# Second part of the output projection in single PSUM banks, later turns of the first group's kept heads, and sample values in slabs

## Chip, cores and metric

The kernel runs on one core of a Trainium2 chip. The metric is the device time of one execution, in microseconds (us). Lower is better.

## The reference, cut to what matters

One decoder layer is computed in fp32 for 2048 prompt tokens and for a sample group of 8 sequences with 8 tokens each; both share the weights. Four retention heads and four HGRN2 heads each carry a state through chunks of 64 tokens; the outputs of the eight heads go through one output projection, the input is added, and a feed-forward part follows.

```python
def mixer(h, pos, s_ret, s_hg, w_in, ret_norm_w, hgrn_norm_w, lb, w_out):
    proj = h @ w_in
    rq, rk, rv, rg, hq, hf, hi, hg = jnp.split(proj, idx, axis=-1)
    ...
    o_r, s_ret_new = chunk_gla(rq, rk, rv, log_g_ret, s_ret)
    o_r = (head_rmsnorm(o_r, ret_norm_w) * gate_r).reshape(B, T, RET_W)
    ...
# chunk_gla, per chunk and head
    o = jnp.einsum('bhts,bhsv->bhtv', A, vb) + jnp.einsum('bhtd,bhdv->bhtv', qb * jnp.exp(b), S)
    S_new = S * jnp.exp(b_last[:, :, 0, :])[..., None] + jnp.einsum('bhsd,bhsv->bhdv', k_dec, vb)
```

The mixer's result is the two groups of heads side by side, times `w_out`; the layer adds its input to it.

## The kernel before

All tokens are cut into three groups: group 0 holds the 64 sample tokens and 512 prompt tokens (T = 576), groups 1 and 2 hold 768 prompt tokens each. A group goes through the mixer in four passes p = 0 to 3, each with one retention head and one HGRN2 head, then through the output projection; the feed-forward part of all groups comes last.

Every fp32 product is made of three matmuls: both operands are cut into a high part and a rest (`hi`, `lo`), and high by high, high by rest and rest by high are added up in PSUM. The cast on ScalarE (ACT) that makes `hi` is L306, the subtraction on VectorE (DVE) that makes `lo` is L314. The matmuls of the plain projections are L448 in `proj`; those of the block products with kept operands are L1844, which `matmul` counts.

PSUM has eight banks. While the mixer runs, the pool `pj` has two buffers of two banks each for the big products, and the pool `mm` has four buffers of one bank for all small ones. After the mixer of the last group the pool `pf` (two buffers of two banks) stands where `mm` was. `tile2()` hands out two buffers of `pf`, then two of `pj`, in turn.

**The output projection** (`out_proj`) of a group has two parts. The first (`residual`) takes the heads of passes 0 to 2 beside the last mixer. The second, which the change touches, runs alone on TensorE (PE): for each of eight column blocks, 12 matmuls into one `pj` tile (128x288 in group 0, 128x384 in the others), then one DVE addition to the first part (L1905), one ACT copy with the weight of the norm (L1906), and two stores, `fres` and `fin` (L1908). With two `pj` buffers, a block can start only when the DVE addition of the block two ahead of it has read its tile.

**Kept heads.** The outputs of passes 0 to 2 are stored (`fo`), and in pass 3 `fetch_heads` loads them again and `cut_heads` turns them: transposes on PE (L1833), then the cut in `hi` on ACT (L1834) and `lo` on DVE (L1835). `later(d, f)` runs `f` after d more ticks; a tick comes after every three (`proj`) or two (`matmul`) products. Those numbers and those of `at` in `mixer` set the order in which the code is issued; a scheduler then sets the order on each engine.

**Sample part of group 0.** In each pass, `sample_values` loads the sample rows of the values three times into one tile (six transfers of 32 KB for the two halves, L1315), casts them and subtracts (L1317). `sample_blocks` spreads them (DVE, L1345), `sample_update` multiplies them with the keys (PE, L1357) and adds the product to the old states (DVE, L1361 for retention, L1364 for HGRN2). The old states of both heads are loaded by `sample_states` (L1291, from `ret_s` and `hg_s`) and read by the matmuls L1306. The running state `S` of the prompt is copied by L1696 and read by L1686. `load()` gives one of the six `ld` buffers, `get()` one of the 44 slabs; both are handed on in a fixed order, so a load waits for the last reader of the buffer that it gets. All transfers named here are issued by SyncE's queue (SP), one after the other: an issue that waits holds up those behind it.

Of the kernel before, what the change touches and what calls it, by code (L numbers as in the profile page):

```python
# [9 lines left out]
F32 = mybir.dt.float32  # L10
# [3 lines left out]
ALU = mybir.AluOpType  # L14

P = 128
# [7 lines left out]
H = 4  # L24
# [70 lines left out]
N_ORDER = (0, 1, 4, 5, 2, 3, 6, 7)  # L95
# [110 lines left out]
class Kernel:  # L206
# [7 lines left out]
    def at(self, when, fn, *a):  # L214
        heapq.heappush(self.agenda, (when, self.n_at, fn, a))
        self.n_at += 1
# [219 lines left out]
            out.append(self.blocks.popleft())  # L436
        return out

    def proj(self, g, blocks, acts, pieces=None):

        pieces = pieces or g.pieces
        T2 = pieces[0][1] - pieces[0][0]
        pj = self.pj.tile([P, 2, 512], F32, tag="pj", name="pj")
        n = len(blocks)
        for j, ((wh, wl), (ah, al)) in enumerate(zip(blocks, acts)):
            for q, (w, a) in enumerate(((wh, ah), (wh, al), (wl, ah))):
                for i, (c0, c1) in enumerate(pieces):
                    self.nc.tensor.matmul(  # L448
                        pj[:, i, :T2], w, a[:, c0:c1],
                        start=j == 0 and q == 0, stop=j == n - 1 and q == 2)  # L450
                self.tick()
        return pj[:, :len(pieces), :T2]

    def cut(self, src, hi, lo, T, lag=0):
        self.tc.keep_in_program_order(self.nc.scalar.copy(hi[:, :T], src[:, :T]))
# [452 lines left out]
    def mix(self, g):  # L908
        nc = self.nc
        if g.ns:  # L910
            g.qm = [self.get(), self.get()]
            for q in g.qm:
                nc.gpsimd.memset(q, 0.0)
        g.o, g.oc = {}, {}
        end = 0
        for p in range(H):
            b = {}
            if self.fast and p == H - 1 and g.i + 1 < len(self.groups):
                self.norm_ahead(self.groups[g.i + 1], g.i == 0)
            (self.project_blocks if g.blocks else self.project)(g, p, b)  # L920
            end = self.mixer(g, p, b, max(self.now, end))
            if p == H - 1:
                for q in range(H - 1):
                    if self.fast:
                        self.later((2, 24, 46)[q] if g.ns else (2, 8, 38)[q], self.fetch_heads, g, q)
                        self.later((22, 44, 66)[q] if g.ns else (22, 40, 64)[q], self.cut_heads, g, q)
                    else:
                        self.later((4, 16, 28)[q], self.cut_heads, g, q)
            (self.values_blocks if g.blocks else self.values_direct if self.fast else self.values)(g, p, b)
# [376 lines left out]
                nc.tensor.matmul(po, g.qm[i][:, s * NS:(s + 1) * NS], s0[i][:, s * P:(s + 1) * P],  # L1306
                                 start=False, stop=i == 1 and s == 3)

    def sample_values(self, g, v):

        nc, out = self.nc, []
        for i in range(2):
            r, w = self.load(), self.getr()
            for t in range(3):
                nc.sync.dma_start(r[32 * t:32 * t + 32, :2 * P], v[32 * i:32 * i + 32])  # L1315
            nc.scalar.copy(w[:96, :2 * P], r[:96, :2 * P])
            nc.vector.tensor_tensor(out=w[64:96, :2 * P], in0=r[64:96, :2 * P], in1=w.bitcast(F32)[64:96, :2 * P], op=ALU.subtract)  # L1317
            out.append(w)
        return out
# [62 lines left out]
    def mixer(self, g, p, b, t0):  # L1382


        nc, T, n0 = self.nc, g.T, g.ns
# [352 lines left out]
        def outs(t):  # L1738
            if n0:
                at(t - 24 if fast else t - 14, sample_load, 0)  # L1740
                at(t - 14, sample_turn, 0)
                at(t - 20, lambda: x.update(vw=self.sample_values(g, b["vrows"])))
                for hd in range(2):
                    at(t - 6 + 8 * hd, lambda hd=hd: x.update({("vm", hd): self.sample_blocks(x["vw"], hd)}))
                at(t + 1, sample, 0)
                at(t + 4, sample_state, 0)
                at(t - 14 if fast else t + 6, sample_load, 1)
                at(t + 6, sample_turn, 1)
                at(t + 10, sample, 1)
                at(t + 13, sample_state, 1)  # L1750
                rows = slice(0, NS)
                at(t + 14, squares, "s", 0, -1, rows)
                at(t + 14, factors, "s", 1, rows)
                at(t + 19, gated, "s", 0, -1, rows)
                t += 15
# [140 lines left out]
    def out_proj(self, g, when, beside, between=lambda: None):  # L1896

        nc, T = self.nc, g.T
        part = self.residual(g, when, beside)
        between()  # L1900
        g.res, g.in_ = (self.dp.tile([P, KB, T], F32, name=self.tag + f"{name}{g.i}") for name in ("res", "in"))
        for n in N_ORDER:
            pj = self.proj(g, self.take(2), g.oc[H - 1])
            r, b = part[n], self.get()
            nc.vector.tensor_tensor(out=self.v2(r, g), in0=pj, in1=self.v2(r, g), op=ALU.add)  # L1905
            nc.scalar.activation(b[:, :T], r[:, :T], AF.Copy, scale=self.vec[:, V_FFN + n:V_FFN + n + 1])  # L1906
            for kept, t in ((g.res, r), (g.in_, b)):
                nc.sync.dma_start(kept[:, n], t[:, :T])  # L1908
        self.flush()
# [555 lines left out]
```

## Time and profile before

| | |
|---|---|
| time, median of 3 runs | 2387.14 us (2385.1 to 2387.51) |
| profiled execution, its own time | 2385.61 us |
| its span in the trace | 2383.8 us (1.8 us lie around it) |
| PE busy | 2351.0 us (99%) |
| DVE busy | 1799.2 us (75%) |
| ACT busy | 1230.7 us (52%) |
| GpSimd (POOL) busy | 148.1 us |
| TensorE clock granted | 0.997 |

The trace gives each instruction with its start, its length and, where its engine was idle before it, what ended the idle time. A line number is that of the kernel before. PE is busy nearly throughout, so the idle time of PE in the trace, piece by piece, is the most that a change of order can win. Lengths of neighbours on DVE and PE overlap a little: what one instruction takes of its engine is the distance of two starts.

### The profile page before, as it was taken

The page shows a single profiled execution, that of the slowest core. Times are in us where ns is not written, and L with a number is a line of the kernel's source. Part 1 is how long each engine was busy: PE and PEld are TensorE (multiplying, and loading weights), DVE is VectorE, ACT ScalarE, POOL GpSimd, SP SyncE. Part 2 cuts the span into 40 slices and gives each one's busy share as a digit, 9 for nine tenths or more (in the row PEclk, how much of TensorE's full clock was granted, in tenths as well). Part 3 has the DMA queues.
Part 4 walks back from the last instruction along what each step waited for, and adds up shares of the span by engine and source line. Part 5 has one row for each costly group of instructions (what it writes and reads, how often), then busy time and mean ns, then how long its engine had stood idle before and what let it go on. Part 6 is the DMA issues. An engine that isn't in the chain of part 4 may idle for free.

```text
span 2383.8 us, 39321 instructions
## 1 busy us (share of the span) xinstructions
PE 2351.0 (99%) x15322; PEld 2309.0 (97%) x15322; DVE 1799.2 (75%) x2299; ACT 1230.7 (52%) x1974; POOL 148.1 (6%) x202
## 2 busy tenths in 40 slices
PE   9999999999999999999999999999999999999998
PEld 8888799999999999999999999999999999999997
DVE  8666777767676766758769997666998786669887
ACT  5555565466654555536455555444544364445443
POOL 4212201010001001000000000000000000000000
PEclk9999999999999999999999999999999999999999
DMA  8888778778858777968677665766655457565541
GB/s 291 287 289 282 257 271 336 266 287 288 321 188 316 290 285 265 320 223 292 225 243 271 230 216 181 243 211 226 240 184 191 152 190 261 198 239 177 204 154 69
DMA packets 232505, 575.60 MB, mean 241 GB/s; under 512 B 24179, under 2 KB 92659, under 8 KB 232310
## 3 DMA queue, kind: packets, MB, share of 16 engines
q1 hardware_dynamic: 232166, 572.98, 68.8%
q8 instruction: 122, 2.00, 0.3%
q14 instruction: 73, 0.60, 0.1%
q10 hardware_dynamic: 144, 0.02, 0.0%
HBM read 419.95 MB, written 151.66 MB: 240 GB/s over the span
## 4 chain that ended last, share of the span: by engine, by line
PE 82%; DVE 2%; ACT 1%; issue 0%; DMA 0%; POOL 0%; SPq 0%; DVEq 0%; ACTq 0%; POOLq 0%
PE pj L1844 35%; PE pf L1844 28%; PE pj L1103 9%; PE pj L448 6%; PE mm L1686 1%; PE mm L1684 1%; PE mm L1692 1%; PE mm L1461 0%; PE mm L1614 0%; PE mm L1372 0%; PE mm L1833 0%; DMA lo<-fki0VA12lo 0%; DVE slab L1905 0%; DVE slab L1940 0%; DVE ld L872 0%
## 5 line engine op out<-in xcount | busy, mean ns | idle before, releaser
L1844 PE MATMUL pj<-slab,hi 128*128 128x384 f32 (+1 forms) x3504 | 853.8, 326 | 2.2 <-ACT hi L306 1.0
L306 ACT CAST hi<-raw 128x1024 fp32r<-128x1024 f32 (+1 forms) x449 | 470.8, 1049 | 683.5 <-PE pj L1844 259.1
L314 DVE TENSOR_TENSOR lo<-raw,hi 128x1024 fp32r<-128x1024 f32 (+1 forms) x449 | 548.8, 1222 | 173.8 <-ACT hi L306 159.5
L1844 PE MATMUL pf<-slab,hi 128*128 128x384 f32 (+1 forms) x2768 | 652.4, 321 | 0.0
L1844 PEld LDWEIGHTS pj<-slab,hi 128*128 128x128 f32 x3504 | 614.6, 188 | 3.4 <-ACT slab L1026 1.3
L1844 PE MATMUL pj<-slab,lo 128*128 128x384 f32 (+1 forms) x1752 | 570.4, 326 | 0.0
L1844 PEld LDWEIGHTS pf<-slab,hi 128*128 128x128 f32 x2768 | 480.7, 188 | 0.1
L1844 PE MATMUL pf<-slab,lo 128*128 128x384 f32 (+1 forms) x1384 | 443.1, 320 | 0.0
L1844 PEld LDWEIGHTS pj<-slab,lo 128*128 128x128 f32 x1752 | 329.4, 188 | 0.0
L1103 PE MATMUL pj<-hi,slab 128*128 128x256 f32 x1344 | 263.1, 288 | 2.8 <-DVE slab L1031 1.8
L448 PE MATMUL pj<-slab,hi 128*128 128x288 f32 (+1 forms) x1280 | 257.0, 316 | 5.6 <-DVE slab L1905 3.3
L1844 PEld LDWEIGHTS pf<-slab,lo 128*128 128x128 f32 x1384 | 260.1, 188 | 0.0
L1103 PEld LDWEIGHTS pj<-hi,slab 128*128 128x128 f32 x1344 | 216.4, 192 | 3.9 <-ACT hi L306 2.0
L448 PEld LDWEIGHTS pj<-slab,hi 128*128 128x128 f32 x1280 | 204.3, 188 | 10.6 <-DVE slab L1905 4.7
L1103 PE MATMUL pj<-lo,slab 128*128 128x256 f32 x672 | 190.8, 284 | 0.4 <-DMA lo<-fki0VA12lo 0.4
L1936 ACT CAST slab<-slab 128x768 fp32r<-128x768 f32 (+1 forms) x192 | 145.5, 779 | 63.7 <-DVE slab L1947 47.4
L1940 DVE TENSOR_TENSOR slab<-slab 128x768 fp32r<-128x768 f32 (+1 forms) x192 | 167.3, 886 | 13.2 <-ACT slab L1936 4.2
L448 PE MATMUL pj<-slab,lo 128*128 128x288 f32 (+1 forms) x640 | 149.5, 314 | 0.2 <-DVE lo L314 0.2
L1103 PEld LDWEIGHTS pj<-lo,slab 128*128 128x128 f32 x672 | 129.4, 193 | 0.6 <-DMA lo<-fki0VA12lo 0.6
L448 PEld LDWEIGHTS pj<-slab,lo 128*128 128x128 f32 x640 | 107.6, 188 | 0.5 <-DVE lo L314 0.5
L2190 DVE TENSOR_TENSOR slab<-pf,slab 128x768 f32<-128x768 f32 (+1 forms) x87 | 76.5, 884 | 24.4 <-PE pf L1844 24.2
L2190 DVE TENSOR_TENSOR slab<-pj,slab 128x768 f32<-128x768 f32 (+1 forms) x79 | 70.1, 888 | 20.5 <-PE pj L1844 20.3
(269 smaller groups left out, 2616.0 us busy)
## 6 DMA issues: line engine op xcount, KB each, us to landing
raw<-w SPq DMA_DIRECT2D x255, 512.0 KB, 4.9
slab<-fu SPq DMA_DIRECT2D x64, 384.0 KB, 5.4
fu<-ld SPq DMA_DIRECT2D x60, 384.0 KB, 3.7
ld<-x SPq DMA_DIRECT2D x40, 384.0 KB, 4.6
ld<-fin SPq DMA_DIRECT2D x28, 384.0 KB, 4.7
slab<-fu SPq DMA_DIRECT2D x32, 288.0 KB, 4.5
fu<-ld SPq DMA_DIRECT2D x30, 288.0 KB, 3.1
fres<-slab SPq DMA_DIRECT2D x16, 384.0 KB, 4.9
```

Source lines behind the costliest of these rows:

```text
L306: self.nc.scalar.copy(self.wts[j][0][:, c], raw[:, c])
L314: self.nc.vector.tensor_tensor(out=lo[:, c], in0=raw[:, c], in1=hi.bitcast(F32)[:, c], op=ALU.subtract)
L448: self.nc.tensor.matmul(pj[:, i, :T2], w, a[:, c0:c1], start=j == 0 and q == 0, stop=j == n - 1 and q == 2)
L1103: self.nc.tensor.matmul(ps[:, tb * 256:(tb + 1) * 256], t, w[:, cols], start=first and kb == j == 0 and tb != 1, stop=kb == KB // 2 - 1 an ...
L1684: nc.tensor.matmul(dst, am(c), b["vc"][c][hd], start=True, stop=first)
L1686: nc.tensor.matmul(dst, qd[:, cols[c]], S, start=False, stop=True)
L1692: nc.tensor.matmul(ps[:, hd * P:(hd + 1) * P], kt[:, c * P:(c + 1) * P], b["vc"][c][hd], start=True, stop=True)
L1844: self.nc.tensor.matmul(*a, **k)
L1936: self.nc.scalar.copy(hi[:, :g.T], B[name][:, :g.T])
L1940: self.nc.vector.tensor_tensor(out=lo[:, :g.T], in0=B[name][:, :g.T], in1=hi.bitcast(F32)[:, :g.T], op=ALU.subtract)
L2190: nc.vector.tensor_tensor(out=r, in0=ps, in1=r, op=ALU.add)
```

## The change

There are three edits, all on the path of the kernel that runs.

```diff
-    def proj(self, g, blocks, acts, pieces=None):
+    def proj(self, g, blocks, acts, apart=False):
-        pieces = pieces or g.pieces
+        pieces = g.pieces
         T2 = pieces[0][1] - pieces[0][0]
-        pj = self.pj.tile([P, 2, 512], F32, tag="pj", name="pj")
+        if apart:
+            banks = [self.mm() for _ in pieces]
+        else:
+            pj = self.bank() if self.pf is None else self.tile2()
+            banks = [pj[:, i] for i in range(len(pieces))]
...
-                        pj[:, i, :T2], w, a[:, c0:c1],
+                        banks[i][:, :T2], w, a[:, c0:c1],
...
-                        self.later((22, 44, 66)[q] if g.ns else (22, 40, 64)[q], self.cut_heads, g, q)
+                        self.later((27, 46, 66)[q] if g.ns else (22, 40, 64)[q], self.cut_heads, g, q)
...
-            r, w = self.load(), self.getr()
+            r, w = self.get() if self.fast and p < H - 1 else self.load(), self.getr()
...
-        for n in N_ORDER:
-            pj = self.proj(g, self.take(2), g.oc[H - 1])
+        for j, n in enumerate(N_ORDER):
+            apart = self.fast and j % 2 == 0 and self.pf is None
+            pj = self.proj(g, self.take(2), g.oc[H - 1], apart)
             r, b = part[n], self.get()
-            nc.vector.tensor_tensor(out=self.v2(r, g), in0=pj, in1=self.v2(r, g), op=ALU.add)
+            for ps, v in zip(pj, (r[:, a:e] for a, e in g.pieces)) if apart else [(pj, self.v2(r, g))]:
+                nc.vector.tensor_tensor(out=v, in0=ps, in1=v, op=ALU.add)
```

First, in the second part of the output projection of groups 0 and 1 the blocks j = 0, 2, 4, 6 go into two `mm` banks and are added by two DVE instructions of half the width; the odd blocks keep `pj`. In group 2, where `pf` is open, the eight blocks take `pf` and `pj` by `tile2()`. Second, in group 0 the turns of the kept heads 0 and 1 come five and two ticks later. Third, in the passes 0 to 2 of group 0 the sample values are loaded into slabs and no longer into `ld` buffers. No matmul is added or taken away; DVE has 8 instructions more (8 whole additions become 16 halves), the other engines have as many as before. The lines behind L440 move by four to six: L448 becomes L452, L1844 L1848, L1905 L1911, L1908 L1914, L1315 L1319, L1291 L1295.

**DVE at the end of group 0's second part.** Before: the additions of the blocks j = 4 to 7 (slab_3600, slab_3645, slab_3696, slab_3763), among instructions that prepare group 1 (L872, L892, L1940).

```order
L1905 TENSOR_TENSOR slab_3600<-pj_3870,slab_3600 128x576
L872 TENSOR_TENSOR ld_3692<-ld_3692,ld_3676 128x768
L1940 TENSOR_TENSOR slab_3882<-ld_3742,slab_3881 128x768
L1905 TENSOR_TENSOR slab_3645<-pj_3902,slab_3645 128x576
L1905 TENSOR_TENSOR slab_3696<-pj_3931,slab_3696 128x576
L1940 TENSOR_TENSOR slab_3919<-ld_3676,slab_3918 128x768
L892 TENSOR_TENSOR ld_3976<-ld_3976,slab_3884 128x768
L1940 TENSOR_TENSOR slab_3946<-ld_3692,slab_3945 128x768
L1905 TENSOR_TENSOR slab_3763<-pj_3957,slab_3763 128x576
L892 TENSOR_TENSOR ld_3977<-ld_3977,slab_3884 128x768
```

After: the same stretch.

```order
L1911 TENSOR_TENSOR slab_3600<-mm_3874,slab_3600 128x288
L1911 TENSOR_TENSOR slab_3600<-mm_3875,slab_3600 128x288
L876 TENSOR_TENSOR ld_3692<-ld_3692,ld_3676 128x768
L1946 TENSOR_TENSOR slab_3887<-ld_3742,slab_3886 128x768
L1911 TENSOR_TENSOR slab_3645<-pj_3908,slab_3645 128x576
L1911 TENSOR_TENSOR slab_3696<-mm_3937,slab_3696 128x288
L1946 TENSOR_TENSOR slab_3925<-ld_3676,slab_3924 128x768
L1911 TENSOR_TENSOR slab_3696<-mm_3938,slab_3696 128x288
L1911 TENSOR_TENSOR slab_3763<-pj_3965,slab_3763 128x576
L1946 TENSOR_TENSOR slab_3953<-ld_3692,slab_3952 128x768
L896 TENSOR_TENSOR ld_3984<-ld_3984,slab_3889 128x768
L896 TENSOR_TENSOR ld_3985<-ld_3985,slab_3889 128x768
```

The additions of j = 4 and j = 6 are now pairs of halves that read `mm`; ahead of the addition of j = 5 the same instructions stand as before, and j = 7 now comes ahead of the second L1940 (now L1946) behind it and of both L892 (now L896). On PE, the matmuls of j = 7 (pj_3965) now stand ahead of those of j = 6 (mm_3937, mm_3938), and group 1's first product (L1848 into pj_3995) follows.

**SP in pass 1 of group 0.** Before: the loads of the old states (`ret_s`, `hg_s`), of the two halves of the sample values (ld_1590, ld_1597), weights, and the stores of cut operands (`fki`) and sums (`fsi`).

```order
L1291 DMA ld_1561<-ret_s 128x4x128
L1291 DMA ld_1563<-ret_s 128x4x128
L1315 DMA ld_1590<-slab_1491 32x256 x3
L1315 DMA ld_1597<-slab_1491 32x256 x3
L248 DMA raw_1829<-w 128x1024
L1291 DMA ld_1625<-hg_s 128x4x128
L248 DMA raw_1945<-w 128x1024
L1291 DMA ld_1627<-hg_s 128x4x128
L384 DMA fki2PA11hi_1630<-hi_1411 128x512
L384 DMA fki2PA11lo_1631<-lo_1412 128x512
L384 DMA fki2PA12hi_1634<-hi_1411 128x512
L384 DMA fki2PA12lo_1635<-lo_1412 128x512
```

After:

```order
L1295 DMA ld_1561<-ret_s 128x4x128
L1295 DMA ld_1563<-ret_s 128x4x128
L1295 DMA ld_1625<-hg_s 128x4x128
L1295 DMA ld_1627<-hg_s 128x4x128
L384 DMA fki2PA11hi_1630<-hi_1411 128x512
L384 DMA fki2PA11lo_1631<-lo_1412 128x512
L1319 DMA slab_1590<-slab_1491 32x256 x3
L384 DMA fki2PA12hi_1634<-hi_1411 128x512
L384 DMA fki2PA12lo_1635<-lo_1412 128x512
L420 DMA fsi2PS1_1652<-raw_1409 128x512
L1319 DMA slab_1597<-slab_1491 32x256 x3
L420 DMA fsi2PS3_1665<-raw_1409 128x512
```

The `hg_s` loads have moved ahead of the sample values; the second half of the values (slab_1597) has moved behind the stores fki2PA12 and fsi2PS1, and the two weight loads behind all of these.

**SP at the end of group 0's second part.** Before: the stores of j = 6 and j = 7, and the loads of the kept operand (hi_3991, lo_3992) for group 1's third product.

```order
L1908 DMA fres0_3765<-slab_3696 128x576
L1908 DMA fin0_3766<-slab_3952 128x576
L822 DMA rt_3938<-fr1_3937 128x6x1
L1908 DMA fres0_3765<-slab_3763 128x576
L1908 DMA fin0_3766<-slab_3971 128x576
L269 DMA hi_3991<-fki0PA12hi_259 128x1024
L269 DMA lo_3992<-fki0PA12lo_260 128x1024
```

After:

```order
L1914 DMA fin0_3766<-slab_3902 128x576
L269 DMA hi_3999<-fki0PA12hi_259 128x1024
L1914 DMA fres0_3765<-slab_3645 128x576
L1914 DMA fin0_3766<-slab_3932 128x576
L824 DMA fr1_3944<-slab_3889 1x768
L1914 DMA fres0_3765<-slab_3696 128x576
L1914 DMA fin0_3766<-slab_3959 128x576
L826 DMA rt_3945<-fr1_3944 128x6x1
L1914 DMA fres0_3765<-slab_3763 128x576
L1914 DMA fin0_3766<-slab_3979 128x576
L269 DMA lo_4000<-fki0PA12lo_260 128x1024
```

The load of the high part (now hi_3999) has moved ahead of the stores of j = 5 (slab_3645); that of the rest (lo_4000) still follows the last store.

More of the change, by code (lines that the diff above doesn't have):

```diff
@@ L448, in proj @@
                     self.nc.tensor.matmul(
-                        pj[:, i, :T2], w, a[:, c0:c1],
+                        banks[i][:, :T2], w, a[:, c0:c1],
                         start=j == 0 and q == 0, stop=j == n - 1 and q == 2)
                 self.tick()
-        return pj[:, :len(pieces), :T2]
+        return [b[:, :T2] for b in banks] if apart else pj[:, :len(pieces), :T2]
     def cut(self, src, hi, lo, T, lag=0):
@@ L1307, in sample_out, with sample_values @@
                                  start=False, stop=i == 1 and s == 3)
-    def sample_values(self, g, v):
+    def sample_values(self, g, v, p):
         nc, out = self.nc, []
         for i in range(2):
-            r, w = self.load(), self.getr()
+            r, w = self.get() if self.fast and p < H - 1 else self.load(), self.getr()
             for t in range(3):
@@ L1741, in outs @@
                 at(t - 14, sample_turn, 0)
-                at(t - 20, lambda: x.update(vw=self.sample_values(g, b["vrows"])))
+                at(t - 20, lambda: x.update(vw=self.sample_values(g, b["vrows"], p)))
                 for hd in range(2):
```

## The prediction

> **What bounds the kernel now.** I read the head of the page first: what is each engine's share, and which engine is the chain that ended last made of.
>
> ```profile
> span 2383.8 us, 39321 instructions
> ...
> PE   9999999999999999999999999999999999999998
> ...
> DVE  8666777767676766758769997666998786669887
> ...
> PE 82%; DVE 2%; ACT 1%; issue 0%; DMA 0%; POOL 0%; SPq 0%; DVEq 0%; ACTq 0%; POOLq 0%
> ```
>
> PE is at nine tenths or more in all slices but the last, and the chain is PE with a little DVE. The change leaves all matmuls as they are. So it can win only idle time of PE, and only at the places that it touches. I therefore asked for PE's waits in three windows: passes 1 to 3 of group 0 (140 to 300 us), the end of group 0's output projection (300 to 360), and that of group 1 (700 to 760).
>
> ```profile
> PE mm L1686 <- DVE S L1696: 1.1, 2, 0.6
> PE mm L1306 <- DMA ld<-hg_s: 1.1, 1, 1.1
> PE mm L1833 <- DMA ld<-fo: 0.8, 2, 0.5
> ```
> ```profile
> PE pj L448 <- DVE slab L1905: 2.7, 3, 1.6
> PE pj L1844 <- ACT hi L306: 1.0, 1, 1.0
> ```
> ```profile
> PE pj L448 <- DVE slab L1905: 0.6, 1, 0.6
> ```
>
> Columns: total us, times, longest. What the edits aim at is small: 2.7 us in group 0's second part, 0.6 in group 1's, 0.8 at the kept heads, 1.1 at the old states of the sample part: **5.2 us**, of 2387.
>
> The table by window (PE, PEld, DVE, ACT, POOL busy, then clock and DMA) says what the 2.7 us consist of.
>
> ```profile
> 300.00:331.60 31.60, 31.21 (x240) 30.47 (x239) 20.41 (x38) 16.56 (x45) 0.90 (x4) 1.00 0.73 256
> 331.60:340.00 8.40, 7.79 (x57) 7.32 (x56) 8.21 (x11) 6.29 (x10) 0.00 (x0) 1.00 0.85 316
> 340.00:350.00 10.00, 7.47 (x50) 6.72 (x49) 10.00 (x14) 9.30 (x16) 0.00 (x0) 1.00 0.72 240
> ```
>
> The second part begins at 331.60 us. From 340 to 350 DVE is busy for 10.00 of 10 us, PE for 7.47. The chain of waits in this window runs through DVE, from instruction to instruction:
>
> ```profile
> 342.96 0.87 DVE slab L1940
> 343.83 0.87 DVE ld L872
> 344.70 0.07 DVE slab L1905
> 344.77 0.52 issue
> 345.28 0.95 DVE ld L872
> 346.23 0.87 DVE slab L1940
> 347.10 0.68 DVE slab L1905
> 347.78 0.04 issue
> 347.82 1.85 PE pj L448 x12
> 349.68 8.16 PE pj L1844 x47
> ```
>
> So the addition that frees a tile is late because DVE is still at the work for group 1, not because the tile is asked for early. More banks shorten the wait only as far as DVE's order brings the needed addition forward.
>
> **Group 0's second part, step by step.** PE's rows at the last two blocks and the first product of group 1, and the DVE rows that say what half an addition costs:
>
> ```profile
> 345.42 0.80 PE L448 MATMUL pj<-slab,hi 128*128 128x288 f32 x4 [1.62 <-DVE slab L1905]
> ...
> 347.82 0.80 PE L448 MATMUL pj<-slab,hi 128*128 128x288 f32 x4 [0.54 <-DVE slab L1905]
> ...
> 349.51 0.51 PE L1844 MATMUL pj<-slab,hi 128*128 128x384 f32 x2
> ```
> ```profile
> 347.02 1.42 DVE L1905 TENSOR_TENSOR slab<-pj,slab 128x576 f32<-128x576 f32 x2
> ```
> ```profile
> L2013 DVE TENSOR_TENSOR slab<-slab 128x384 f32<-128x384 f32 x12 | 6.7, 554 | 0.2
> L2013 DVE TENSOR_TENSOR slab<-slab 128x288 f32<-128x288 f32 x4 | 1.8, 454 | 0.0
> L1905 DVE TENSOR_TENSOR slab<-pj,slab 128x576 f32<-128x576 f32 x8 | 5.9, 750 | 0.0
> ```
>
> Two whole additions of 750 ns take 1.42 us together, so neighbours overlap by 0.08, and one takes 0.67 of DVE. A 128x288 addition of SBUF operands takes 454 ns. I take the same for the half that reads PSUM, since the width sets it; less 0.08 that is 0.37, two halves 0.75: 0.08 us more per split block. (Bounds: 0, if halves overlap more, and 0.16 without any overlap.)
>
> The wait that then ends last is that of group 1's first product (pj_3995). It takes the `pj` tile of j = 5, whose addition in DVE's order still stands behind the same instructions as before. Before, that addition begins at 347.02 and takes 0.67, to 347.69; three split blocks ahead of it add 3 x 0.08 = 0.24, so 347.93. In the rows before, the last block starts at 347.82, 0.13 behind the 347.69 that freed its tile. So the product starts at 347.93 + 0.13 = 348.06 instead of 349.51: **1.45 us won**. PE must be ready by then. Its blocks need 1.6 us each, from 331.60 on, and the sums between them (L671, L672) some 0.9: 345.3 by itself. The second half of j = 6 waits for the half addition of j = 4, which DVE's rows put at 344.62 + 0.75 + 2 x 0.08 = 345.5, and ends at 346.4. That wait lies inside the other. The gain's upper bound is that PE runs freely to the end: 349.51 - 345.3 = 4.2. The lower bound is 0, if the two `mm` banks, which the sums share, come free late.
>
> Does the next wait eat it? PE's third product of group 1 waits at 358.96 for its kept operand, whose loads are issued behind the last store:
>
> ```profile
> 358.96 0.59 PE L1844 MATMUL pj<-slab,hi 128*128 128x384 f32 x2 [0.96 <-ACT hi L306]
> ```
> ```profile
> 350.95 0.75 DVE L1905 TENSOR_TENSOR slab<-pj,slab 128x576 f32<-128x576 f32 x1
> ```
> ```profile
> 353.79 0.38 SPq L1908 DMA_DIRECT2D fin<-slab  x1
> 354.26 0.41 SPq L269 DMA_DIRECT2D hi<-fki0PA12hi  x1
> 354.76 0.38 SPq L269 DMA_DIRECT2D lo<-fki0PA12lo  x1
> ```
>
> The releaser named, a cast, is 0.96 us of it; a load of 354.26 that must land first is the other candidate. In SP's new order the high part leaves ahead of the stores of j = 5. The rest still follows the last store, whose addition now ends at 347.93 + 0.37 + 0.87 + 0.37 + 0.67 = 350.21 (half, L1946, half, whole) instead of 350.95 + 0.67 = 351.62: 1.4 earlier, as much as PE. So this wait stays near its size and the gain holds. I take **-1.4**.
>
> The Trainium skill, "VectorE: DVE Perf Modes", section "The TRN2 errata — SBUF-src ops pay a fixed extra latency per instruction", speaks against halves: it gives an fp32 addition as (N + 151)/0.96 ns and advises at least 512 elements. For 576 columns that is 757 ns and for 288 457 ns, and this trace agrees (750 and 454). The rule charges the 151 cycles, 0.16 us, to each further instruction, and the term would then be -1.45 + 3 x 0.16 - 0.24 = -1.2 instead of -1.4; the starts in this trace show half of it hidden.
>
> **Group 1's and group 2's second part.** Here DVE is less full.
>
> ```profile
> 712.74 0.98 PE L448 MATMUL pj<-slab,hi 128*128 128x384 f32 x4 [0.62 <-DVE slab L1905]
> ```
>
> One wait of 0.62; every second block now has banks of its own and the next tile is two blocks older. I take **-0.6** (0 to -0.8). Group 2 has no such wait in the list, so 0.
>
> **Kept heads.**
>
> ```profile
> 255.46 0.64 PE L1833 MATMUL mm<-con,ld 64*128 64x64 f32 x3 [0.35 <-DMA ld<-fo]
> 256.60 0.64 PE L1833 MATMUL mm<-con,ld 128*128 128x128 f32 x3 [0.50 <-DMA ld<-fo]
> ```
>
> The two waits are for the loads of head 0. Five ticks are 15 matmuls; at the 0.13 us between starts of the 128x288 matmuls above they are 2 us, more than both together: **-0.85** (0, if the later turn pushes its casts into a queue, to -1.1). The later two heads shift by 2 and 0 ticks and showed no wait.
>
> **Sample values.** In pass 1 the `hg_s` loads wait behind the values; the issue rows of SP, with the wait that PE shows at the other end:
>
> ```profile
> 135.32 4.02 SPq L1315 DMA_DIRECT2D ld<-slab  x6
> 139.38 0.58 SPq L248 DMA_DIRECT2D raw<-w  x1
> 140.75 0.37 SPq L1291 DMA_DIRECT2D ld<-hg_s  x1
> ...
> 145.98 1.44 SPq L420 DMA_DIRECT2D fsi2PS<-raw  x1
> ```
> ```profile
> 145.56 0.62 PE L1357 MATMUL mm<-slab 96*128 96x512 f32 x2
> ...
> 150.07 1.06 PE L1306 MATMUL mm<-ld,slab 128*64 128x128 f32 x8 [1.05 <-DMA ld<-hg_s]
> ```
>
> After, `hg_s` leaves about where the values left (135.3), 5 us earlier: -1.05. But the second half of the values now leaves behind fsi2PS, whose turn came at 145.98. Half of the value transfers (4.02/2 = 2.0 us) and two weight loads (0.58 each) have gone from ahead of that store: 3.2 us sooner, 142.8, if nothing else holds the queue. What comes behind it, from these rows:
>
> ```profile
> ld<-slab SPq DMA_DIRECT2D x3, 32.0 KB, 2.0
> ```
> ```profile
> 142.20 0.42 DVE L1317 TENSOR_TENSOR slab<-ld,slab 32x256 fp32r<-32x256 f32 x1
> ...
> 147.32 0.68 DVE L1345 TENSOR_TENSOR slab<-slab,con 96x512 fp32r<-96x512 f32 x1
> ```
>
> The store's 1.44, two more transfers of 0.67, 2.0 to landing, the cast (an estimate of 0.4, by L1317), 0.42 and 0.68: 149.1, and up to 0.5 more if DVE is at another addition. PE reached L1357 at 145.56; with the matmuls that the new order puts ahead I estimate 148.6. I take a new wait of 1.0 and 0.4 for the copies of S behind it (the row L1686 above, 1.1 in two waits, says that they have no slack): **+1.4** (0, to +4.6 if the store's turn stays at 145.98). Pass 1 is then +0.35 in sum. Passes 0 and 2 move the same way, without a `hg_s` wait to win; their matmuls L1357 also stand later in PE's order. I take 0 (-0.5 to +2.3). The weight loads that fall back are needed many casts later, so nothing there.
>
> **Sum.** -1.4 - 0.6 - 0.85 + 0.35 = -2.5. Against the profiled execution's own 2385.6 that is 2383.1; the median of the runs lies 1.5 higher, so 2384.6 on the scale of the median.
>
> **Rivals.**
> - *All four waits go*, 5.2 us and 1.2 more of group 0's stall that the list leaves out (4.2 instead of 2.7, less the 0.3 for halves), and no wait comes in pass 1: -6.4, 2380.7 on the median's scale, as all times here. For it: group 0's waits all name L1905, and the banks are there. Against it: DVE's 10.00 of 10 us.
> - *The sample matmuls wait* (slower). The second half of the values is queued on SP behind a store that itself waits for DVE. If this store keeps its turn at 145.98, PE waits 3.2 us more at L1357 in pass 1, 4.2 in all, and 0.4 for the copies of S; the same in pass 2, by half (2.3) or in full (4.6): +6.9 to +9.2. With the gains of 1.4, 0.6, 0.85 and 1.05 that is +3.0 to +5.3: 2390.1 to 2392.4. For it: SP is one queue, and the new rows stand there. Against it: what has left the queue ahead of the store. It decides from a turn of some 143 us on; at 145 it eats all gains.
> - *The gain is taken back at once*: group 1's third product keeps its start at 358.96, since its cast and loads are late whatever PE does. Then -1.4 falls away: 2386.0.
> - By the page's rule the sum is -2.3 and the time 2384.8.
>
> **How the numbers follow.** A change of 0.2% (4.8 us) is about what a measurement of this kernel can tell from no change. I give the forecast 0.5, all waits gone 0.24, gain taken back 0.1, the slower case 0.16. Only the second lies over 0.2% faster; of the slower case the upper end lies beyond the bound on the other side (2391.9), joined by what passes 0 and 2 may add to it. Faster 0.25 (the second, and a little of the forecast's spread), same 0.61, slower 0.14. The range goes from just below the case of all waits gone into the lower half of the slower case: 2380.3 to 2391.0.
>
> **What would show it.** In the profile after: L452 <- L1911 in the window 300 to 360 with about 0.8 us, and a new row L1848 <- L1911 of about 2 us; group 1's first L1848 1.4 us closer to the start of the second part; no L1306 <- hg_s; no L1837 <- fo; a new L1361 <- DVE (L1349) of 1 us near 149. If the DVE row of the window 340 to 350 is no longer full, the first step is wrong. If L1361 or L1690 wait for 3 us or more in passes 1 and 2, the slower rival holds.

## The result and the profile after

The change makes the kernel slower: **2393.27 us** median of 10 runs (2389.16 to 2396.59) against 2387.32 us (10 runs, 2384.22 to 2388.8), a ratio of 1.0026 with the 95% interval 1.0018 to 1.0034. The profiled execution took 2394.31 us.

The head of the page and the chain, as before:

```profile
span 2392.5 us, 39318 instructions
...
DVE  8666777767776666748769997666998786669887
...
PE 84%; DVE 2%; DMA 2%; ACT 1%; issue 0%; POOL 0%; SPq 0%; DVEq 0%; ACTq 0%; POOLq 0%
```

The span is 8.7 us longer in these two executions, and the slices hardly differ: no engine became the bound, PE just waits more often. Where it does, the starts of the same matmul in both traces show. The table gives seven places and how much later each comes than before.

| matmul (line of before) | before, us | after, us | later by | added since the row above |
|---|---|---|---|---|
| L1183, ahead of pass 0's sample part | 60.21 | 60.05 | -0.16 | |
| L1187, behind pass 0 | 130.01 | 132.72 | +2.71 | **+2.87** |
| L1329, behind pass 1 | 206.78 | 210.43 | +3.65 | +0.94 |
| L1833, first turn of the kept heads, behind pass 2 | 255.46 | 263.36 | +7.90 | **+4.25** |
| L448, start of group 0's second part | 331.60 | 339.07 | +7.48 | -0.42 |
| L1844, group 1's first product | 349.51 | 355.51 | +6.00 | **-1.48** |
| end of the span | 2383.8 | 2392.5 | +8.7 | +2.7 |

So the edit of the output projection does win its 1.5 us, and the passes 0 and 2 of group 0 lose 6.7: 2.87, and 3.83 from 206.78 to 331.60. (The second edit itself moves the row of 255.46 back. In e2 and e4 below, which have it, that place is 0.8 us later against before than 331.60 is; in e1 and e3, which lack it, the two differ by 0.1 at most.) The 0.94 of pass 1 can't be told from nothing by this table: e2, e3, e4, e8 and e10, whose code in the passes 0 and 1 is that of before, move between 130.01 and 206.78 by -1.9 to +0.2 us against it, and by 0.3 at most in pass 0.

The waits of PE after, by window: 60 to 140, 140 to 200, 200 to 300, and 300 to 367 us.

```profile
PE mm L1688 <- ACT dump L1720: 1.3, 2, 0.8
PE pj L1191 <- ACT slab L1202: 1.0, 1, 1.0
PE pj L1191 <- DVE slab L1002: 0.6, 1, 0.6
PE mm L1361 <- DVE slab L1349: 0.2, 1, 0.2
```
```profile
PE mm L1361 <- ACT slab L961: 1.6, 1, 1.6
PE mm L1688 <- ACT dump L1720: 0.5, 1, 0.5
```
```profile
PE mm L1333 <- ACT slab L1330: 1.5, 2, 1.0
PE pj L1187 <- DVE slab L1002: 0.8, 1, 0.8
PE mm L1690 <- ACT slab L1445: 0.7, 1, 0.7
PE mm L1361 <- DVE ld L1365: 0.6, 1, 0.6
```
```profile
PE pj L1848 <- DVE slab L1911: 1.7, 1, 1.7
PE pj L1848 <- ACT slab L1030: 1.3, 1, 1.3
PE mm L452 <- DVE slab L1911: 0.6, 1, 0.6
```

The wait for `hg_s` and that for `fo` have gone from the first lines of their windows, as they were to. In their place stand eleven waits of 0.5 to 1.6 us between 60 and 300 us; eight of them name ACT and three DVE. Group 1's window, 700 to 760, no longer has L452 behind L1911.

What makes ACT late, its own rows show. Before, passes 0, 1 and 2, with the idle time ahead of an instruction and what ended it in brackets:

```profile
74.75 0.87 ACT L1316 CAST slab<-ld 96x256 fp32r<-96x256 f32 x2 [3.42 <-DMA ld<-slab]
75.52 1.36 ACT L955 ACTIVATE slab<-slab 128x512 f32<-128x512 f32 x2
```
```profile
139.39 0.41 ACT L1316 CAST slab<-ld 96x256 fp32r<-96x256 f32 x1 [0.37 <-DMA ld<-slab]
140.70 0.41 ACT L1316 CAST slab<-ld 96x256 fp32r<-96x256 f32 x1 [0.90 <-DMA ld<-slab]
141.01 1.36 ACT L955 ACTIVATE slab<-slab 128x512 f32<-128x512 f32 x2
```
```profile
210.52 0.41 ACT L1316 CAST slab<-ld 96x256 fp32r<-96x256 f32 x1 [0.95 <-DMA ld<-slab]
210.83 1.36 ACT L955 ACTIVATE slab<-slab 128x512 f32<-128x512 f32 x2
```

After, first pass 1 up to the first cast, then pass 0, then pass 2 (L1316 is now L1320, the gates L955 are L959):

```profile
146.26 0.40 ACT L1320 CAST slab<-slab 96x256 fp32r<-96x256 f32 x1 [4.54 <-DMA slab<-slab]
```
```profile
75.18 0.41 ACT L1320 CAST slab<-slab 96x256 fp32r<-96x256 f32 x1 [3.68 <-DMA slab<-slab]
81.76 0.27 ACT L1720 ACTIVATE dump<-mm 64x128 bf16<-64x128 f32 x1 [6.17 <-PE mm L1310]
...
82.03 0.39 ACT L1320 CAST slab<-slab 96x256 fp32r<-96x256 f32 x1
82.33 1.36 ACT L959 ACTIVATE slab<-slab 128x512 f32<-128x512 f32 x2
```
```profile
215.06 0.40 ACT L1320 CAST slab<-slab 96x256 fp32r<-96x256 f32 x1 [3.70 <-DMA slab<-slab]
216.26 1.05 ACT L306 CAST hi<-raw 128x1024 fp32r<-128x1024 f32 x1 [0.80 <-PE mm L1310]
217.44 0.41 ACT L1320 CAST slab<-slab 96x256 fp32r<-96x256 f32 x1
217.75 1.37 ACT L959 ACTIVATE slab<-slab 128x512 f32<-128x512 f32 x2
```

Before, nothing stands between the two casts, and the gates of HGRN2 (L955 to L957) follow. After, the second half of the values comes so late that other instructions stand between the two casts, and these wait for PE: in pass 0 ACT sits idle for 6.17 us ahead of an activation that needs a matmul of the sample part (L1310), with the second cast and all gates queued behind it. The gates begin at 82.33 instead of 75.52 in pass 0, 6.8 us later, and at 217.75 instead of 210.83 in pass 2, 6.9 us later, of which 3.65 had been lost by 206.78. DVE's spread of the values (L1345) and PE's update (L1357) follow the second cast.

### The profile page after: what moved, and what is told of

Its sections match the earlier page's. It is cut to its first block, busy times and chain, and to the rows that moved or that the text cites. A ratio compares the mean times of both kernels' runs of the same rounds, so it can differ in the third digit from the quotient of the medians.

```text
span 2392.5 us, 39318 instructions
## 1 busy us (share of the span) xinstructions
PE 2352.1 (98%) x15322; PEld 2307.4 (96%) x15322; DVE 1801.6 (75%) x2307; ACT 1230.3 (51%) x1974; POOL 153.2 (6%) x202
## 4 chain that ended last, share of the span: by engine, by line
PE 84%; DVE 2%; DMA 2%; ACT 1%; issue 0%; POOL 0%; SPq 0%; DVEq 0%; ACTq 0%; POOLq 0%
PE pj L1848 36%; PE pf L1848 28%; PE pj L1107 9%; PE pj L452 6%; PE mm L1690 1%; PE mm L1696 1%; PE mm L1688 1%; DMA lo<-fki0VA12lo 1%; PE mm L1376 0%; PE mm L1618 0%; PE mm L1465 0%; DMA ld<-x 0%; PE mm L1837 0%; PE pf L452 0%; PE mm L452 0%
## 5 line engine op out<-in xcount | busy, mean ns | idle before, releaser
L1848 PE MATMUL pj<-slab,hi 128*128 128x384 f32 (+1 forms) x3504 | 853.9, 326 | 4.1 <-ACT slab L1030 1.9
L306 ACT CAST hi<-raw 128x1024 fp32r<-128x1024 f32 (+1 forms) x449 | 470.6, 1049 | 687.5 <-PE pj L1848 260.2
L1848 PE MATMUL pf<-slab,hi 128*128 128x384 f32 (+1 forms) x2768 | 652.3, 321 | 0.0
L1848 PEld LDWEIGHTS pj<-slab,hi 128*128 128x128 f32 x3504 | 614.7, 188 | 5.2 <-ACT slab L1030 2.6
L1848 PE MATMUL pj<-slab,lo 128*128 128x384 f32 (+1 forms) x1752 | 570.5, 326 | 0.0
L1848 PEld LDWEIGHTS pf<-slab,hi 128*128 128x128 f32 x2768 | 480.7, 188 | 0.1
L1848 PE MATMUL pf<-slab,lo 128*128 128x384 f32 (+1 forms) x1384 | 443.1, 320 | 0.0
L1848 PEld LDWEIGHTS pj<-slab,lo 128*128 128x128 f32 x1752 | 329.3, 188 | 0.0
L1848 PEld LDWEIGHTS pf<-slab,lo 128*128 128x128 f32 x1384 | 260.1, 188 | 0.0
L452 PE MATMUL pj<-slab,hi 128*128 128x288 f32 (+1 forms) x1184 | 235.7, 315 | 2.3 <-ACT slab L715 1.4
L452 PEld LDWEIGHTS pj<-slab,hi 128*128 128x128 f32 x1184 | 188.1, 188 | 5.5 <-ACT slab L715 1.7
L1946 DVE TENSOR_TENSOR slab<-slab 128x768 fp32r<-128x768 f32 (+1 forms) x192 | 167.2, 886 | 13.2 <-ACT slab L1942 4.4
L452 PE MATMUL pj<-slab,lo 128*128 128x288 f32 (+1 forms) x592 | 139.4, 314 | 0.2 <-DVE lo L314 0.2
L452 PEld LDWEIGHTS pj<-slab,lo 128*128 128x128 f32 x592 | 99.6, 188 | 0.5 <-DVE lo L314 0.5
```

Of the source, the lines that this page charges most:

```text
L306: self.nc.scalar.copy(self.wts[j][0][:, c], raw[:, c])
L452: self.nc.tensor.matmul(banks[i][:, :T2], w, a[:, c0:c1], start=j == 0 and q == 0, stop=j == n - 1 and q == 2)
L1848: self.nc.tensor.matmul(*a, **k)
L1946: self.nc.vector.tensor_tensor(out=lo[:, :g.T], in0=B[name][:, :g.T], in1=hi.bitcast(F32)[:, :g.T], op=ALU.subtract)
```

## The experiments

Theory A, formed from this profile, was that the sample values make the loss; theory B, its rival, that the banks and turns do. Later C and D divide A: the order on SP and what hangs on it (C), or the scarcity of slabs (D). Times are medians; each ratio is to the kernel before, run on the same chip.

| run | us | before, us | ratio, 95% interval |
|---|---|---|---|
| e1, only slabs | 2395.54 | 2386.82 | 1.0032 (1.0021 to 1.0043) |
| e2, only heads | 2385.73 | 2386.82 | 0.9995 (0.9986 to 1.0004) |
| e3, only banks | 2383.82 | 2386.82 | 0.9988 (0.9979 to 0.9997) |
| e4, banks and heads | 2385.69 | 2386.82 | 0.9990 (0.9981 to 0.9999) |
| e5, slabs, pinned order | 2390.69 | 2386.77 | 1.0012 (1.0003 to 1.0021) |
| e6, whole change, pinned order | 2385.69 | 2386.77 | 0.9996 (0.9987 to 1.0005) |
| e7, values in tiles of their own, 43 slabs | 2387.33 | 2386.77 | 1.0001 (0.9992 to 1.0011) |
| e8, all blocks in small banks | 2385.26 | 2386.77 | 0.9992 (0.9983 to 1.0001) |
| e9, slabs, casts on GpSimd | 2394.33 | 2386.83 | 1.0030 (1.0022 to 1.0039) |
| e10, 43 slabs | 2390.88 | 2386.83 | 1.0017 (1.0008 to 1.0026) |
| e11, e7 with banks and heads | 2386.87 | 2386.83 | 0.9995 (0.9986 to 1.0004) |
| e12, e7 with the values later | 2398.52 | 2387.49 | 1.0047 (1.0033 to 1.0061) |

And at the places of the table above, how much later than before each comes in the profiled executions (us):

| | 60 | 130 | 207 | 255 | 332 | 350 | 366 |
|---|---|---|---|---|---|---|---|
| the change | -0.2 | 2.7 | 3.7 | 7.9 | 7.5 | 6.0 | 6.1 |
| e1 | 0.3 | 2.0 | 5.5 | 9.4 | 9.5 | 9.5 | 9.5 |
| e2 | 1.5 | 1.4 | -0.5 | 0.6 | -0.2 | -0.2 | -0.2 |
| e3 | 1.3 | 1.3 | -0.1 | 0.1 | 0.0 | -1.5 | -1.3 |
| e4 | 2.0 | 2.0 | 1.1 | 2.8 | 2.0 | 0.5 | 0.7 |
| e5 | 0.0 | 1.5 | 1.1 | 2.3 | 2.2 | 2.2 | 2.8 |
| e6 | -0.3 | 1.4 | 1.4 | 2.9 | 2.1 | 0.6 | 3.6 |
| e7 | 2.3 | 2.4 | 0.9 | 0.0 | -1.1 | -1.1 | -1.1 |
| e8 | -0.3 | -0.6 | -1.5 | -1.9 | -1.9 | - | 0.9 |
| e9 | -0.4 | 1.1 | 2.6 | 6.5 | 6.6 | 6.6 | 6.6 |
| e10 | 0.1 | -0.2 | 0.0 | 0.1 | 1.2 | 1.2 | 1.6 |
| e11 | 0.1 | 0.4 | -1.1 | -1.6 | -3.8 | -4.5 | -2.8 |
| e12 | 3.6 | 6.8 | 7.1 | 13.9 | 13.6 | 13.6 | 15.7 |

The last column is a product L1844 at 366.01; in e8 group 1's first products stand between the blocks, so that its column 350 has no value.

A part of these numbers is the granted clock of TensorE, which drops to half in short stretches (last section). It was 0.72 from 9 to 15 us in e2, e3, e4 and e7 and 0.51 from 9 to 16 in e12, and these five are the late ones in the column 60. It was 0.51 as well from 153 to 160 us in e1 (pass 1), from 227.6 to 234.5 in e12 (pass 2), from 349.5 to 356.5 in e6 and from 359 to 366 in e8, which can cost up to 3.4 us each time (half of 6.8, an estimate). In the change's trace it is 1.00 throughout these stretches.

### e1 to e4: which edit

e1 has the third edit alone, e2 the second, e3 the first, e4 the first two; the edits are those of the diff.

> Only the third edit, the sample values in slabs. Theory A (the loss comes from the sample values: the second half of them lands late and whatever stands behind it in PE's order waits, and the DVE and ACT chains behind that): 6 to 8 us slower than before, with waits at L1357 and at the small products L1684 to L1692 in the passes 0 to 2. Theory B (the loss comes from the order that the other edits set, by the banks taken from the small products or the later turns): within 1 us of before.

> Only the second edit, the kept heads of group 0 turned five and two ticks later. Theory A: 0 to 0.9 us faster than before, since the two waits for the loads fo of 0.8 us go. Theory B: 2 to 4 us slower, since the later turns push the work of the last pass back.

> Only the first edit, every other block of the second part in two small banks. Theory A: 1.5 to 2.5 us faster (1.4 in group 0, 0.6 in group 1), with L448 still waiting for DVE in group 0. Theory B: 1 to 3 us slower, because the small banks, late handed back, hold up group 1's first products and its mixer between 360 and 700 us.

> The first and the second edit, sample values in ld buffers as before. Theory A: 2 to 3.4 us faster than before. Theory B: 3 to 6 us slower, nearly the whole loss of the change.

The slabs cost 0.32%, some 7.6 us: as much as the whole change (0.26%), as far as the intervals tell. The banks gain 0.12% (0.03 to 0.21), and no run with the first two edits alone is slower. Theory A holds and B falls. The heads alone gain nothing that can be told: the interval of e2 spans 1, and in its trace the two waits for `fo` are gone, but smaller ones for DVE stand in their place, among them:

```profile
PE mm L1833 <- DVE slab L1835: 0.3, 1, 0.3
PE mm L1372 <- DVE slab L1835: 0.2, 1, 0.2
```

In e3, PE's rows at the end of group 0's second part:

```profile
345.30 0.54 PE L452 MATMUL mm<-slab,hi 128*128 128x288 f32 x2 [0.65 <-DVE slab L1911]
...
348.06 0.62 PE L1848 MATMUL pj<-slab,hi 128*128 128x384 f32 x2 [1.70 <-DVE slab L1911]
```

They are the waits that the prediction worked out, and the second ends at 348.06 us, as it said.

### e5 and e6: the order on SP

```diff
-                nc.sync.dma_start(r[32 * t:32 * t + 32, :2 * P], v[32 * i:32 * i + 32])
+                self.tc.keep_in_program_order(nc.sync.dma_start(r[32 * t:32 * t + 32, :2 * P], v[32 * i:32 * i + 32]))
...
-            self.nc.sync.dma_start(s[:, :512].rearrange("p (s v) -> p s v", v=P),
-                                   src[4 * i:4 * i + 4, h].rearrange("s d v -> d s v"))
+            self.tc.keep_in_program_order(self.nc.sync.dma_start(s[:, :512].rearrange("p (s v) -> p s v", v=P),
+                                   src[4 * i:4 * i + 4, h].rearrange("s d v -> d s v")))
```

e5 is e1 with this, e6 the whole change with this.

> Slabs for the sample values as in e1, but the transfers of the values and of the old states keep their order of the code on SyncE, so that the values leave ahead of the hg_s loads, as in the kernel before. Theory C (the loss is the order on SP: the scheduler puts the hg_s loads and the stores of the cut operands ahead of the values, the values land some 6 to 8 us later, and ScalarE, whose casts of them stand ahead of the gate activations L955 to L957, passes the delay on): the loss of e1 goes, 0 to 1.5 us faster than before, and the second cast L1316 of pass 1 within 2 us of its place before, 140.7. Theory D (the loss is the rotation of the slabs: six more per pass make other work wait for its buffers): still 4 us or more slower than before.

> All three edits with the same pinned order. Theory C: as banks and heads together, 1 to 4 us faster than before. Theory D: 1 to 4 us slower than before.

The pins take back most of the loss, 1.0032 to 1.0012 in the one pair and 1.0026 to 0.9996 in the other, but not all: e5 lies between the two theories, some 2.9 us slower than before (0.7 to 5.0). e6 can't be told from the kernel before, where C asked for 1 to 4 us; its trace is 0.6 us late at 350 and 3.6 at 366, behind its stretch of half clock. In pass 2 the loss falls from 3.9 to 1.2 us. In pass 1 it falls from 3.6 to none, but up to 3.4 of e1's 3.6 are its clock; in the pair of the change and e6 it falls from 0.9 to none. In pass 0 it stays: 1.5 after e1's 1.7. There the pins did not bring the old order back. They hold the values ahead of the `hg_s` loads alone, and the second half now leaves behind a store, at 76.30, where all six transfers had left by 73.09 before:

```profile
75.87 0.33 SPq L420 DMA_DIRECT2D fsi1PS<-raw  x1
76.30 1.79 SPq L1315 DMA_DIRECT2D slab<-slab  x3
```

So 1.5 of the 2.2 us that e5 is late at 332 arise where its values are late again.

One expectation failed: the second cast of pass 1 was to be within 2 us of 140.7.

```profile
145.82 0.40 ACT L1316 CAST slab<-slab 96x256 fp32r<-96x256 f32 x1 [5.27 <-DMA slab<-slab]
146.48 0.41 ACT L1316 CAST slab<-slab 96x256 fp32r<-96x256 f32 x1 [0.25 <-DMA slab<-slab]
146.79 1.37 ACT L955 ACTIVATE slab<-slab 128x512 f32<-128x512 f32 x2
```

It is 5.8 us late, 4.2 of them beyond the 1.5 that this execution had lost by 130, and the pass loses nothing by it against this trace of before. So the values have some 4 us of slack in pass 1; the change's second cast, at 148.88, is 5.5 us late by the same count, and e1's, at 148.55, 5.9. The two halves run together again here, without another instruction between them.

### e7, e10 and e11: is it the slabs?

```diff
+            self.sv = ctx.enter_context(tc.tile_pool(name="sv", bufs=2))
...
-            r, w = self.load(), self.getr()
+            r, w = self.sv.tile([96, 2 * P], F32, tag="sv", name="sv") if self.fast else self.load(), self.getr()
...
-SIZES = {True: (44, 8, 3), False: (43, 4, 5)}
+SIZES = {True: (43, 8, 3), False: (43, 4, 5)}
```

e7 has all of this, e10 the last line alone, e11 is e7 with the first two edits of the change.

> Only the sample values changed, in two small tiles of their own and neither in ld nor in slabs; to make room there are 43 slabs instead of 44. Theory C: the order on SP is that of the kernel before with the hg_s loads free of the ld buffers, so 0 to 1.5 us faster than before, if one slab less costs nothing. Theory D: within 1 us of before as well, or slower by what the missing slab costs; it is told apart by e5.

> The kernel before with 43 slabs instead of 44 and nothing else changed. If the slabs are so short that the six more per pass make others wait (theory D as the rest of the loss that e5 left), this costs 1 us or more as well. If their number is not what counts, within 0.5 us of before. It is also the control for e7.

> The first and the second edit with the sample values in two small tiles of their own and 43 slabs. By the sums so far (e4 -1 to -2, e7 +0.5, the hg_s wait of 1.05 gone): 1 to 4 us faster than before, not clearly ahead of e3 or e4.

One slab less costs 0.17% (0.08 to 0.26), 4 us. In its trace the first new waits stand in pass 3, for the spread values and the states:

```profile
PE mm L1357 <- DVE slab L1345: 1.3, 2, 0.7
PE mm L1306 <- DMA ld<-hg_s: 0.6, 1, 0.6
```

So slabs are short, and theory D may have a part in what e5 left beside pass 0; no run shows it, nor which buffer that would be. Against its control e10, e7 is 3.6 us faster in the medians: with neither `ld` nor slabs taken by the values, the wait for `hg_s` goes and none comes. PE's list of 140 to 200 us in e7 holds only L1685 behind ACT (0.4) and L1687 behind DVE (0.3). But the wait for `hg_s` is no fixed price: with the code of before in that pass, it is 0.9 in e10, 0.3 in e4, and not in the lists of e2, e3 and e8.

By the places e7 gains 3.4 us between 60 and 332 us, of which 1.5 fall between 130 and 207, where e2 and e3 gain 1.9 and 1.4 with the code of before. The median ends where it began; that the missing slab takes the gain back is the likely reading, and not shown. e11, of which 1 to 4 us were asked, can't be told from before: its interval spans 1. Its trace is 4.5 us ahead at 350 and 1.2 at the end.

### e8: all blocks in small banks

```diff
-            apart = self.fast and j % 2 == 0 and self.pf is None
+            apart = self.fast and self.pf is None
```

e8 is e3 with this.

> Only the first edit, but with all eight blocks of the second part of groups 0 and 1 in two small banks each. If VectorE's order sets the end of group 0's second part, nothing more is won: within 1 us of e3, and the first product of group 1 starts at 348.1 to 348.8, since now all additions ahead of it are halves. If tiles are short, it starts 1 us or more ahead of e3's 348.06.

The second came, and did not last: with the `pj` tiles free, the scheduler puts group 1's first products between the blocks, the first of them ahead of 340 us, and the waits for L1911 go. The next limit takes it back, the load that stands behind the last stores on SP:

```profile
360.72 0.69 PE L1848 MATMUL pj<-slab,lo 128*128 128x384 f32 x1 [4.01 <-DMA lo<-fki0PA12lo]
```

At 366 us it is 2.8 us worse off than at 332, where e3 is 1.3 better; but some 2.6 of the 2.8 can be the half clock that e8 had then (5.3 us from 360.72 to 366, an estimate). The median, 2385.26, is not ahead of e3's 2383.82. So tiles were short, in the sense that PE had other work to do, and the gain did not outlast the wait for that load.

### e9 and e12: what carries the lateness

```diff
-            nc.scalar.copy(w[:96, :2 * P], r[:96, :2 * P])
+            (nc.gpsimd.tensor_copy if self.fast and p < H - 1 else nc.scalar.copy)(w[:96, :2 * P], r[:96, :2 * P])
```

e9 is e1 with this. e12 is e7 with the other call time:

```diff
-                at(t - 20, lambda: x.update(vw=self.sample_values(g, b["vrows"])))
+                at(t - 8, lambda: x.update(vw=self.sample_values(g, b["vrows"])))
```

> As e1 (values in slabs, order left to the scheduler), but the two casts of the values in the passes 0 to 2 are copies on GpSimd instead of ScalarE. The values land as late as in e1. Theory C with ScalarE as the carrier: the gate activations L955 to L957 no longer stand behind the casts, so in pass 1 they start 5 us or more ahead of e1's 148.87, and some 3 us or more of the loss of 8 go; the wait of L1357 stays. If the delay goes by VectorE and L1357 alone: no gain against e1, at most 1 us.

> As e7 (values in two tiles of their own, 43 slabs), but sample_values is called 8 ticks instead of 20 ahead of the sample part, so that on SP in pass 1 both halves leave behind the hg_s loads, the four fki2PA stores and the store fsi2PS1, as the second half does in the change. On ScalarE the gates now stand ahead of the casts. No slab is taken by the values. Theory C (the late values make the loss, whatever buffer they are in): 3 to 6 us slower than e7, with a wait at L1357 in pass 1 of 1 us or more. If the slabs' rotation makes the loss: within 1 us of e7.

In e9 the gates of pass 1 start at 144.84, 4.0 us ahead of e1's 148.87 (5 were asked), and the median is not better. The passes 0 and 2 lose 1.5 and 4.0 us, e1's 1.7 and 3.9. Pass 1 loses 1.5 and e1's 3.6, but up to 3.4 of e1's are its clock, and the change with its casts on ACT loses 0.9. So no gain by the earlier gates is shown. For the passes 0 and 2 the run tells nothing of ACT: with no cast ahead of them, the gates still start as late, at 82.14 (e1 82.75) behind an activation that waits for PE, and at 216.06 (e1 219.42, 3.0 of it lost earlier) behind a cast L306 ahead of which ACT sat idle for 4.82 us. Which engine carries the lateness to PE stays open.

e12 is the worst of all, 1.0047, with not one slab more than e7 and with the gates ahead of the casts on ACT: the values alone, whose casts run 10 to 12 us later than in e7, cost 11 us, where C asked for 3 to 6.

```profile
PE mm L1358 <- DVE slab L1346: 5.4, 5, 1.5
```

L1358 is the update, L1346 the spread of the values. That late values can make such a loss without the slabs is shown. They are later here than in the change, though (in pass 1 the casts are at 153.11 and 155.06, against 146.26 and 148.88 with 4.1 us less lost by 130), so the run does not show that the change's own lateness suffices; for that speaks e6, where the order alone is pinned and the loss goes.

## Why the prediction was wrong

**The step that failed** is the one on the sample values outside pass 1: "Passes 0 and 2 move the same way, without a `hg_s` wait to win; their matmuls L1357 also stand later in PE's order. I take 0 (-0.5 to +2.3)." They cost 2.87 and 3.83 us. Pass 1, which was worked out, was put at +0.35 and came to +0.94. With 6.7 us in place of that 0, the sum of -2.5 becomes +4.2, which is 2391.3 on the median's scale; the measured 2393.27 is 2.0 above it.

- *The reason given held, and was not enough*: the matmuls L1357 (now L1361) do stand late there and wait for no more than 0.24 us in pass 0 and 0.60 in pass 2. The loss comes at other matmuls, which wait for what ACT and DVE do behind the late values: L1688 (0.49 and 0.79) and L1191 (0.61) behind pass 0, L1690 (0.70) and L1187 (0.75) behind pass 2. The same mechanism was followed through several engines where a wait was to be won, and to one matmul where none was.
- *What the working left out* is what else stands on ACT. It followed the second half of the values on SP, through the cast to DVE and L1357. It did not ask what is queued behind the cast on its engine, or what is put ahead of it: in pass 0 the transfer leaves SP at 72.97 to 75.47 behind no store that waits, yet the cast runs at 82.03, behind an activation that waits for PE. That this is the way to PE is read from the rows; e9 did not bear it out.
- *GpSimd was left out too*: the late spreads (L1349) meet GpSimd's L1367, twice each in the passes 1 and 2, and then take 1.4 to 1.5 us instead of 0.68 (last section). The first of them, at 151.41, ends 0.14 us ahead of the matmul L1361 of 153.09, whose wait of 1.62 had been put at 1.0. (The list names the gate L961, which ends 0.03 ahead of it.)
- *That pass 1 came near its term is in part luck*: the 1.05 to be won at `hg_s` are that one execution's. Against e2, e3, e4 and e8, whose code there is that of before, the change loses 1.9 to 2.8 us in pass 1.
- *The slower rival* named the right place and the right queue, with a chance of 0.16, and its 2.3 to 4.6 for pass 2 hold the 3.83. Its condition was not the cause: the store fsi2PS went at 144.31 in the change, 141.6 without the 2.7 us that this trace was late by then, so ahead of its 143, and pass 1 lost only 0.94. In the passes 0 and 2 the values leave ahead of the pass's stores fsi. The sign set for it, 3 us or more at L1361 or L1690 in the passes 1 and 2, did not come either: 1.62, 0.60 and 0.70.

```profile
144.31 0.32 SPq L420 DMA_DIRECT2D fsi2PS<-raw  x1
144.92 2.57 SPq L1319 DMA_DIRECT2D slab<-slab  x3
```

- *Group 0's second part* (-1.4) was right in mechanism and size: -1.48 in the change, -1.47 in e3 and e4, with DVE again full in the matching stretch:

```profile
346.60:356.60 10.00, 7.66 (x51) 7.03 (x51) 10.00 (x15) 8.26 (x14) 0.00 (x0) 1.00 0.71 246
```

- *What half an addition takes*: two halves from 352.24 to the next start at 352.97, 0.73, where 0.75 was put and the Trainium skill's rule ("VectorE: DVE Perf Modes", section "The TRN2 errata — SBUF-src ops pay a fixed extra latency per instruction") charges 0.91 for the two. A single half reads PSUM in 0.44 us; the rule's 457 ns agree with the length, and the starts hide part of it.

```profile
352.24 0.81 DVE L1911 TENSOR_TENSOR slab<-mm,slab 128x288 f32<-128x288 f32 x2
352.97 0.95 DVE L876 TENSOR_TENSOR ld<-ld 128x768 f32<-128x768 f32 x1
...
355.37 0.44 DVE L1911 TENSOR_TENSOR slab<-mm,slab 128x288 f32<-128x288 f32 x1
```

- *The next wait* (L1844 at 358.96) stayed about as it was: 1.0 for ACT before, 1.3 for ACT after. "The gain is taken back at once" did not happen in the change; in e8 it did.
- *Group 1* (-0.6): its wait is gone from the list. What e3 gains as a whole, 3 us in the medians with an interval of 0.7 to 5.0, holds both terms and doesn't tell them apart.
- *Kept heads* (-0.85): the waits for `fo` went, and e2 can't tell whether the time came; DVE's cut L1835 was the next to be waited for (0.3 and 0.2).

Of the span's last 2.7 us, between 350 us and the end, the cause is not settled. PE waits there for loads like fki0VA12lo, 0.4 us before, 0.8 in e3 and 1.6 after. In e1, which leaves that part as it was, the places lose 3.6 between 366 and 602 us, of which 1.7 can be the clock (0.57 from 402 to 406).

## What to carry to other kernels

A buffer taken from another pool moves the transfer in the queue, and what must be priced is every engine that this transfer's readers stand on, in each place where it recurs, not only where the profile shows a wait. A late operand can be expensive twice: by its reader, and by what the scheduler then puts ahead of that reader on its engine (6.17 us of idle ACT in pass 0). Where a step is put at nothing, name the slack that hides it and its size; here it was some 4 us in pass 1, and the change used 5.5. And before two traces are compared place by place, compare their clocks.

## What the runs showed of the hardware

VectorE is slowed by GpSimd at the sample part. In e1, GpSimd's L1363 ran from 150.61, and the pair L1345 on VectorE took 2.14 us; before, with no L1363 beside it, the same pair took 1.28.

```profile
150.87 2.14 DVE L1345 TENSOR_TENSOR slab<-slab,con 96x512 fp32r<-96x512 f32 x2
```
```profile
150.61 1.25 POOL L1363 TENSOR_TENSOR ld<-ld,slab 128x512 f32<-128x512 f32 x1 [3.55 <-PE mm L1306]
```
```profile
143.26 1.28 DVE L1345 TENSOR_TENSOR slab<-slab,con 96x512 fp32r<-96x512 f32 x2
```

All traces say the same of the single L1345: it takes 0.68 to 0.69 us in the 201 records in which no GpSimd addition of 128x512 (L1363) that started ahead of it still runs, and 1.36 to 1.58 us in all 23 in which one does. Before, that happens once, at 296.10; in the change five times, four of them in the passes 1 and 2. No run varied it by itself.

The granted clock of TensorE drops to half for 3.4 or 6.8 us at a time, at other places in each execution, and once more in the last 8 to 12 us of each. In e1 this fell into pass 1; PE ran 27 matmuls there, where the change's trace has 44 in the same window. The rows give PE, PEld, DVE, ACT and POOL busy, then the clock and DMA:

```profile
153.00:160.00 7.00, 7.00 (x27) 5.80 (x27) 6.57 (x10) 3.14 (x10) 3.03 (x3) 0.51 0.76 274
```
```profile
153.00:160.00 7.00, 6.91 (x44) 5.83 (x45) 6.97 (x10) 3.21 (x12) 3.72 (x3) 1.00 0.72 258
```

At 60 us, ahead of the edits' places, the five traces with such a stretch near 10 us are 1.3 to 3.6 us late, and the other eight lie within -0.4 and 0.3. So a difference between two profiled executions is an edit's only where their clocks agree, and even then not below some 2 us in pass 1 (e2's -1.9 with the code of before). What sets these stretches, no run here shows.
